# Six adaLN vectors move out of the two mixers and into the FFN blocks of a two-layer hybrid decoder

## The chip, the cores and the metric

The kernel runs on one NeuronCore of one Trainium2 chip. The metric is the time of one execution in microseconds (us); the time before is the median of 3 runs. An engine takes its instructions in order: PE is TensorE's matmul (PEld its weight load), DVE VectorE, ACT ScalarE, POOL GpSimd, SP the engine that issues most DMAs.

## The reference, cut to what matters

Two layers of three sub-layers: FFN, mixer, FFN. Each sub-layer has three vectors of 1024 numbers, shift, scale and gate, that come out of one condition vector `c`:

```python
for l in range(DEPTH):                       # 2 layers
    mod = (silu(c) @ ada_w[l] + ada_b[l]).reshape(Bn, N_SUB, 3, D_MODEL)
    shift, scale, gate = mod[:, :, 0], mod[:, :, 1], mod[:, :, 2]
    # sub-layer s = 0 and 2: y = swiglu(h, w1, w3, w2); s = 1: y = hybrid_mixer(h, ...)
    h = x * (1 + scale[:, s]) + shift[:, s]
    x = layer_norm(ALPHA * x + weight * (1 + gate[:, s]) * y, ln_g[l, s], ln_b[l, s])
```

`x` is 512 x 1024, the FFN is 2816 wide, everything is f32. That makes 18 vectors (2 layers, 3 sub-layers, 3 each), each a product of the 1024 numbers silu(c) with a 1024 x 1024 piece of `ada_w` (4 MB).

## The kernel before, in words

**Products.** A weight tile of 128 x 1024 is loaded (`raw`), cut into a high part (`whi`, ACT, L103) and the rest (`wlo`, DVE, L105), and each product takes three matmuls, high x high, low x high, high x low (L121 to L123, in `mm3`). Activations are cut in the same way (`hT_hi` and `hT_lo`).

**FFN block** (`ffn`). 22 tiles of hidden units in two halves of 11. For each tile an up step: two weight tiles, 48 matmuls of 512 columns (`h`), and the gated product on ACT and DVE (L310 to L316). Then the down steps: for each hidden tile one weight tile times the gate row `G` (L101), cut and used in 24 matmuls (`y`). `bg()` is called after each step: it makes the next pieces of background work.

**Mixer** (`mixer`). Input projections (`tA`, `tB`, `pj`), the state-space part, compression (`hid`), then the attention stage: for 24 units (`p`, query block, branch) scores `S`, a softmax on DVE and ACT, four transposes into `tp` (L921), a copy of `tp` by ACT into `pt` (L923), and the product of `pt` with the values into `op` (L931). A list of `jobs` (projections, then the output product `y`) is put between them by `tick`; `part` and `rest` are the output product and the closing norm of a block of 128 tokens.

**adaLN vectors** (`ada_vec`). A vector takes 8 loads of 512 KB (in_ada_w) and 8 products with reduction on DVE (L156, a "dot"): a tile of weights times the row `csil` (silu of c, made by `silu_c` on ACT L146 and DVE L147). Its 8 columns are then joined with the bias. A gate vector goes to DRAM and comes back as a row `G` on all partitions (L190, L192); scale and shift go with the norm's gains into `GA` and `BB` (`next_par`, L204 to L206), which `spread` uses to make the next sub-layer's `hT` (ACT L226 and L228, DVE L224 and L229). The first two vectors are made in `feed`; the other 16 in the order of the list `order`: gate of a sub-layer, then scale and shift of the next. `share` says how many of them each sub-layer makes: 4, 3, 3, 3, 3. In an FFN block a vector's tiles are buffers of the pool `bp` (8 of 4 KB a partition, also used by `lg`, `lb`, `G`, `z`), loaded one ahead; in a mixer they are the same 4 `raw` buffers as the weights'. `make_bias` (the table of position biases, which the mixer reads as `T` from DRAM, `lane`) is run in the first FFN ahead of the last vector there. The mixer forgets `csil` before it begins and makes it again in the attention stage.

**Order of work.** A scheduler lays the instructions of each engine in a fixed order when the program is built: an instruction may be far ahead of the place where the code calls it. PE follows that order and waits where an operand is late.

Of the kernel before, what the change touches and what calls it, by code (L numbers as in the profile page):

```python
# [51 lines left out]
def kernel(ctx: ExitStack, tc: tile.TileContext, a: dict, out: bass.AP,  # L52
                             subs=((0, 0), (0, 1), (0, 2), (1, 0), (1, 1), (1, 2))):
# [23 lines left out]
    def big(s):  # L77
        return bp.tile([128, 1024], F32, tag="b", name=nm(s))

    def tiny(s, n, dt=F32):  # L80
        rot = s in ("mx", "sm", "fc", "st", "mv", "rs", "nr", "gst", "ss")
        return (t4 if rot else t1).tile([128, n], dt, tag=f"t_{s}", name=nm(s))
# [4 lines left out]
    def load(dst, src):  # L87
        nc.sync.dma_start(dst, src)

    def bcast_row(src, n):  # L90
        return bass.AP(tensor=src.tensor, offset=src.offset, ap=[[0, 128], [1, n]])
# [51 lines left out]
    def silu_c():  # L143
        csil, c_th = big("csil"), big("cth")
        load(csil, bcast_row(a["c"][0], 1024))
        S.activation(c_th, csil, AF.Tanh, scale=0.5)  # L146
        V.scalar_tensor_tensor(csil, c_th, 1.0, csil, op0=ALU.add, op1=ALU.mult)  # L147
        cond["c"] = csil
# [10 lines left out]
    def ada_fetch(l, s, j, k):  # L159
        raw = big("raw0")  # L160
        load(raw, a["ada_w"][l, s * 3 + j, k])
        return raw

    def ada_vec(l, s, j, ahead=None, follow=None):
        acc, ab = tiny(nm("mod"), 8), tiny("ab", 8)
        load(ab, a["ada_b"][l, s * 3 + j])
        for k in range(8):
            if ahead is None:
                raw = wp.tile([128, 1024], F32, tag="raw", name=nm("raw"), bufs=4)
            else:  # L170
                raw = ahead.pop(0)
                if k < 7:
                    ahead.append(ada_fetch(l, s, j, k + 1))
                elif follow:
                    ahead.append(ada_fetch(*follow, 0))
            ada_dot(acc, raw, l, s * 3 + j, k, ahead is None)
            yield
        if j == 0:
            V.tensor_add(acc, acc, ab)
        else:  # L180
            V.scalar_tensor_tensor(acc, acc, 1.0, ab, op0=ALU.add, op1=ALU.add)
        mods[l, s, j] = acc
        if j == 2:
            d = dram.tile([1, 1024], F32, tag=nm("mod"), name=nm("mod"))
            load(bass.AP(tensor=d.tensor, offset=d.offset, ap=[[1, 128], [128, 8]]), acc)
            mods[l, s, j] = d

    def gate_par(l, s, P):
        g = P["G"] = big("G")
        load(g, bcast_row(mods[l, s, 2][0], 1024))  # L190
        if s != 1:
            V.tensor_scalar(g, g, 0.25, None, op0=ALU.mult)  # L192

    def norm_par(l, s, P):
        P["lg"], P["lb"] = big("lg"), big("lb")
        load(P["lg"], bcast_row(a["ln_g"][l, s], 1024))
        load(P["lb"], bcast_row(a["ln_b"][l, s], 1024))

    def next_par(l, s, nl, ns, P):
        GA, BB = P["GA"], P["BB"] = tiny("GA", 8), tiny("BB", 8)  # L200
        load(GA, a["lng_c"][l, s])
        load(BB, a["lnb_c"][l, s])
        sc, sh = mods[nl, ns, 1], mods[nl, ns, 0]
        V.tensor_mul(GA, sc, GA)  # L204
        V.tensor_mul(BB, sc, BB)
        V.tensor_add(BB, BB, sh)  # L206
# [227 lines left out]
    def mixer(l, P, last, lane, bg, gate_params, norm_params):  # L434
# [440 lines left out]
        def score(p, qb, br, rate):  # L875
            if p not in lanes:
                lane_load(p)
            if br == 0:
                return score_c(p, qb)
            nk = (qb + 1) * 128  # L880
            per = 2 if nk <= 256 else 1
            qs = slice(qb * 128, (qb + 1) * 128)
            mx, sm = tiny("mx", 4), tiny("sm", 4)
            pr = []
            for e, (g, i) in enumerate(heads(p)):
                if e % per == 0:
                    ps, pt = bank("S", "S"), slab("P", "P")
                cols = slice(e % per * nk, (e % per + 1) * nk)
                o, w = ps[:, cols], pt[:, cols]
                PE.matmul(o, Q[g, i][:, qs], K[br][0][g][:, :nk], start=True, stop=False)  # L890
                PE.matmul(o, Q[g, i][:, qs], K[br][1][g][:, :nk], start=False, stop=True)  # L891
                m = mx[:, e:e + 1]
                V.tensor_tensor_reduce(out=w, in0=o, in1=lanes[p][e][:, 512 - nk:], scale=-1.0, scalar=3.0e38,
                                       op0=ALU.add, op1=ALU.min, accum_out=m)
                S.activation(w, w, AF.Exp, bias=m, scale=-1.0, accum_out=sm[:, e:e + 1])
                pr.append(w)
                tick(rate)
            factor(sm, p, qb, br)
            for e in range(4):
                if (br, e) in ACT_SCALE:  # L900
                    S.activation(pr[e], pr[e], AF.Copy, scale=sm[:, e:e + 1])
                else:
                    V.tensor_scalar(pr[e], pr[e], sm[:, e:e + 1], None, op0=ALU.mult)
            return pr
# [100 lines left out]
                    jobs.pop(0)  # L1005
            credit[0] = min(credit[0], 1)

        silu_c()
        probs = [score(*u, TICK_0) for u in units[:LOOK]]
        for n, (p, qb, br) in enumerate(units + [(2, 0, 0)]):  # L1010
            if n + LOOK < len(units):
# [55 lines left out]
    lane = []  # L1067

    order = []
    for n, (l, s) in enumerate(subs):  # L1070
        order.append((l, s, 2))
        if n + 1 < len(subs):
            order += [(*subs[n + 1], 1), (*subs[n + 1], 0)]
    share = {0: 4, 1: 3, 2: 3, 3: 3, 4: 3}

    def need(*key):
        if key not in mods:
            if "c" not in cond:
                silu_c()
            for _ in ada_vec(*key):  # L1080
                pass

    def make_bg(n, P):
        l, s = subs[n]
        items = [k for k in order if k not in mods][:share.get(n, 0)]
        total = 9 * len(items) + (8 if n == 0 else 0) + (s != 1)
        slots = {0: 34, 1: 18, 4: 18}.get(n, 36)
        early = 10 if n == 0 else 0
        done = [0, 0]

        def parts():
            ahead = None
            if s != 1 and items:
                ahead = [ada_fetch(*items[0], 0)]
                yield
            for key, follow in zip(items, items[1:] + [None]):
                yield from ada_vec(*key, ahead, follow)
                if key == (l, s, 2):
                    gate_par(l, s, P)
                if n + 1 < len(subs) and key == (*subs[n + 1], 0):  # L1100
                    next_par(l, s, *subs[n + 1], P)
                yield
                if n == 0 and key == items[-2]:
                    yield from make_bias()

        gen = parts()

        def bg(more=False):
            done[0] += 0 if more else 1
            k = early // 2  # L1110
            even = 2 * done[0] if done[0] <= k else early + (done[0] - k) * (total - early) // (slots - k)
            want = done[1] + 1 if more else min(total, even)
            while done[1] < want:
                done[1] += 1
                next(gen, None)

        return bg

    for n, (l, s) in enumerate(subs):
        last = n == len(subs) - 1  # L1120
        P = {}

        def params():
            norm_par(l, s, P)
            if (l, s, 2) in mods:
                gate_par(l, s, P)
            if not last and (*subs[n + 1], 0) in mods:
                next_par(l, s, *subs[n + 1], P)

        if s == 1:  # L1130
            if not lane:
                for _ in make_bias():
                    pass
            need(l, s, 2)
            cond.clear()
            mixer(l, P, last, lane, make_bg(n, P), lambda: gate_par(l, s, P), lambda: norm_par(l, s, P))
        else:
            if share.get(n) and "c" not in cond:
                silu_c()
            after_mixer = n > 0 and subs[n - 1][1] == 1  # L1140
            ffn(l, s, P, last, make_bg(n, P), (2, 0) if after_mixer and QORDER[0] == 3 else (0, 2), params,
                feed if n == 0 else None)
# [87 lines left out]
```

## Time and profile before

| what | value |
|---|---|
| median of 3 runs | 2078.81 us (2078.62 to 2080.05) |
| the profiled execution's own time | 2078.53 us |
| its span | 2076.8 us, mean granted TensorE clock 0.998 |
| first FFN block, up to the first mixer | 0 to about 388 us |
| first mixer (attention from about 512) | 388 to about 694 us |
| second and third FFN block | 694 to 1045, 1045 to 1410 us |
| second mixer (attention from about 1534) | 1410 to about 1716 us |
| last FFN block | 1716 to 2077 us |

How to read the profile: a row of the stretches gives busy time and number of instructions (in brackets) of PE, PEld, DVE, ACT and POOL, then the granted TensorE clock, the share of the DMA engines' time and GB/s. A row of the timeline gives start, duration, engine, line, operation, what it writes and reads, form, number, and in square brackets idle time before it with what ended it. Matmuls overlap: each is shown with about 0.39 us, and one starts every 0.23 us. So PE's pace is read from starts and not from durations. "issue" is time in which the engine waited for nothing that the profile shows.

### The profile page before, as it was taken

How to read it: one execution, taken by the hardware profiler on the slowest of the kernel's cores; microseconds unless marked ns; L12 is line 12 of the kernel's file. 1: busy time of each engine (PE TensorE's matmuls, PEld its weight loads, DVE VectorE, ACT ScalarE, POOL GpSimd, SP SyncE). 2: the span in 40 equal slices, each digit the busy share in tenths (PEclk: the TensorE clock that was granted, in tenths of full speed). 3: DMA queues.
4: the chain of work that ended last, by engine and by line, in shares of the span. 5: the costliest groups of instructions: out<-in, count | busy, mean ns of one | idle time of the engine just before them, and what ended most of it. 6: DMA issues, size and time to landing. Idle time of an engine off the chain costs nothing.

```text
span 2076.8 us, 25951 instructions
## 1 busy us (share of the span) xinstructions
PE 2037.8 (98%) x10024; PEld 1652.0 (80%) x10024; DVE 1330.7 (64%) x2425; ACT 770.2 (37%) x1352; POOL 27.8 (1%) x43
## 2 busy tenths in 40 slices
PE   6999999999999999999999999999999999999997
PEld 5888888887666888888888888888776678888886
DVE  6784455778898875334696534468788984444454
ACT  3321223525556422222343222235356673222322
POOL 0000000000000000000000000000000000000000
PEclk9999999999999999999999999999999999999999
DMA  9662633235353763332566333143254523233321
GB/s 359 225 232 83 213 122 124 74 99 173 126 169 92 260 201 108 93 100 61 172 231 185 93 100 98 65 144 102 92 172 129 176 79 125 81 112 93 100 92 41
DMA packets 93144, 280.26 MB, mean 135 GB/s; under 512 B 19251, under 2 KB 23603, under 8 KB 93020
## 3 DMA queue, kind: packets, MB, share of 16 engines
q1 hardware_dynamic: 92348, 275.95, 40.6%
q0 software_dynamic: 672, 2.64, 0.4%
q8 instruction: 79, 1.29, 0.3%
q14 instruction: 45, 0.37, 0.1%
HBM read 276.41 MB, written 4.76 MB: 135 GB/s over the span
## 4 chain that ended last, share of the span: by engine, by line
PE 90%; DVE 5%; ACT 2%; issue 1%; DMA 1%; POOL 0%; SPq 0%; POOLq 0%; ACTq 0%
PE h L121 15%; PE h L122 15%; PE h L123 15%; PE y L121 8%; PE y L123 8%; PE y L122 8%; PE pj L121 3%; PE pj L122 3%; PE pj L123 3%; PE op L931 3%; PE tp L921 2%; PE S L890 1%; DVE raw L156 1%; PE S L891 1%; PE hid L624 1%
## 5 line engine op out<-in xcount | busy, mean ns | idle before, releaser
L103 ACT CAST whi<-raw 128x1024 fp32r<-128x1024 f32 (+1 forms) x306 | 316.8, 1046 | 719.4 <-issue 353.8
L121 PE MATMUL h<-hT_hi,whi 128*128 128x512 f32 (+1 forms) x1488 | 559.1, 377 | 4.5 <-ACT hT_hi L1064 4.4
L122 PE MATMUL h<-hT_lo,whi 128*128 128x512 f32 (+1 forms) x1488 | 559.1, 376 | 0.0
L123 PE MATMUL h<-hT_hi,wlo 128*128 128x512 f32 (+1 forms) x1488 | 558.9, 376 | 0.0
L105 DVE TENSOR_TENSOR wlo<-raw,whi 128x1024 fp32r<-128x1024 f32 (+1 forms) x306 | 369.4, 1215 | 232.8 <-ACT whi L103 232.4
L121 PEld LDWEIGHTS h<-hT_hi,whi 128*128 128x128 f32 x1488 | 280.1, 188 | 56.0 <-ACT hT_hi L1064 5.4
L123 PEld LDWEIGHTS h<-hT_hi,wlo 128*128 128x128 f32 x1488 | 280.4, 188 | 50.8
L122 PEld LDWEIGHTS h<-hT_lo,whi 128*128 128x128 f32 x1488 | 280.5, 188 | 50.5 <-DVE hT_lo L1065 0.2
L121 PE MATMUL y<-whi,ghi 128*128 128x512 f32 x576 | 224.1, 389 | 0.0
L122 PE MATMUL y<-wlo,ghi 128*128 128x512 f32 x576 | 224.1, 389 | 0.0
L123 PE MATMUL y<-whi,glo 128*128 128x512 f32 x576 | 224.1, 389 | 0.0
L156 DVE CUSTOM_DVE_ANT_0 raw<-raw,csil 128x1024 f32<-128x1024 f32 x144 | 173.7, 1218 | 22.9 <-DMA raw<-in_ada_w_dram 22.4
L312 DVE TENSOR_TENSOR th<-th,h 128x512 f32<-128x512 f32 x88 | 60.2, 685 | 147.3 <-PE h L123 146.9
L101 DVE TENSOR_TENSOR raw<-raw,G 128x1024 f32<-128x1024 f32 x86 | 104.9, 1221 | 66.8 <-DMA raw<-in_w_dram 66.3
L123 PEld LDWEIGHTS y<-whi,glo 128*128 128x128 f32 x576 | 108.1, 188 | 22.5
L121 PEld LDWEIGHTS y<-whi,ghi 128*128 128x128 f32 x576 | 108.1, 188 | 22.5
L122 PEld LDWEIGHTS y<-wlo,ghi 128*128 128x128 f32 x576 | 108.1, 188 | 22.4
L121 PE MATMUL pj<-hT_hi,whi 128*128 128x512 f32 x288 | 117.3, 407 | 0.0
L122 PE MATMUL pj<-hT_lo,whi 128*128 128x512 f32 x288 | 113.7, 395 | 0.0
L123 PE MATMUL pj<-hT_hi,wlo 128*128 128x512 f32 x288 | 113.3, 393 | 0.0
L315 ACT CAST ghi<-th 128x512 fp32r<-128x512 f32 x88 | 54.5, 620 | 145.7 <-DVE th L312 145.7
L311 DVE SCALAR_TENSOR_TENSOR th<-th,h 128x512 f32<-128x512 f32 x88 | 59.9, 681 | 44.9 <-ACT th L310 44.8
(291 smaller groups left out, 2552.4 us busy)
## 6 DMA issues: line engine op xcount, KB each, us to landing
raw<-in_w_dram SPq DMA_DIRECT2D x264, 512.0 KB, 3.6
raw<-in_ada_w_dram SPq DMA_DIRECT2D x144, 512.0 KB, 5.5
raw<-in_wS_dram SPq DMA_DIRECT2D x36, 512.0 KB, 3.5
raw<-in_cw_dram SPq DMA_DIRECT2D x16, 512.0 KB, 3.7
raw<-in_wo_dram SPq DMA_DIRECT2D x16, 512.0 KB, 4.2
T<-lane SPq DMA_DIRECT2D x16, 256.0 KB, 3.7
lg<-in_ln_g_dram SPq DMA_DIRECT2D x6, 512.0 KB, 4.6
lb<-in_ln_b_dram SPq DMA_DIRECT2D x6, 512.0 KB, 3.8
```

Of the source, the lines that this page charges most:

```text
L101: V.tensor_mul(raw, raw, gain)
L103: S.copy(hi[:, :n], raw[:, :n])
L105: V.tensor_sub(lo[:, :n], raw[:, :n], hi[:, :n].bitcast(F32))
L121: PE.matmul(o, lh, rh, start=first, stop=False)
L122: PE.matmul(o, lh, rl, start=False, stop=False)
L123: PE.matmul(o, ll, rh, start=False, stop=last)
L156: V.tensor_tensor_reduce(out=raw, in0=raw, in1=cond["c"], scale=0.5, scalar=0.0, op0=ALU.mult, op1=ALU.add, accum_out=acc[:, k:k + 1])
L311: V.scalar_tensor_tensor(th, th, 1.0, h1, op0=ALU.add, op1=ALU.mult)
L312: freed[0] = V.tensor_mul(th, th, h3).ins
L315: S.copy(hi, th)
L921: PE.transpose(tp[0:n, e * 128:(e + 1) * 128], pr[e][:, kb * 128:kb * 128 + n], ident)
L931: PE.matmul(op[r, :], v, pt[0:n, g * 256:(g + 1) * 256], start=(br == 0), stop=(br == 2 and kb == qb))
```

## The change

`share` becomes 6, 5, 5 for the first, second and third FFN block; both mixers make none, and the last FFN block makes none as before. The order of the list stays. So these vectors change place (layer, sub-layer, kind):

- scale and shift of (0, 2): from the first mixer to the first FFN block; `make_bias` now runs after five vectors there and not after three.
- gate of (0, 2): from the first mixer to the second FFN block, which uses it itself.
- scale of (1, 1): from the third FFN block to the second.
- gate of (1, 2), scale and shift of (1, 2): from the second mixer to the third FFN block.

The mixer no longer calls `silu_c`; the second FFN block does, since it finds no `csil`. `GA` and `BB` for the sub-layer after a mixer are now made in the mixer's step for the norm's parameters.

```diff
@@ mixer
-        silu_c()
         probs = [score(*u, TICK_0) for u in units[:LOOK]]
@@
-    share = {0: 4, 1: 3, 2: 3, 3: 3, 4: 3}
+    share = {0: 6, 2: 5, 3: 5}
@@
             need(l, s, 2)
             cond.clear()
-            mixer(l, P, last, lane, make_bg(n, P), lambda: gate_par(l, s, P), lambda: norm_par(l, s, P))
+
+            def last_params():
+                norm_par(l, s, P)
+                next_par(l, s, *subs[n + 1], P)
+
+            mixer(l, P, last, lane, make_bg(n, P), lambda: gate_par(l, s, P), last_params)
```

On PE the order within the FFN blocks stays but for the two small matmuls of `make_bias`; in the attention stages it changes. Two places, before and now.

First PE in the first mixer's attention, the same unit of scores in both (`tp` transposes of scaled scores `P`, `op` the product with values `vS`, `S` scores, `y` output product). Before:

```order
L921 MATMUL tp_5156<-cst,P_4958 128x128
L931 MATMUL op_5083<-pt_5144,vS_2879 64x256 x2
L921 MATMUL tp_5156<-cst,P_4964 128x128
L921 MATMUL tp_5156<-cst,P_4970 128x128
L921 MATMUL tp_5156<-cst,P_4976 128x128
L921 MATMUL tp_5165<-cst,P_4958 128x128
L921 MATMUL tp_5165<-cst,P_4964 128x128
L921 MATMUL tp_5165<-cst,P_4970 128x128
L921 MATMUL tp_5165<-cst,P_4976 128x128
L121 MATMUL y_5327<-whi_4632,hT_hi 128x512
L931 MATMUL op_5083<-pt_5161,vS_2879 64x256 x2
L931 MATMUL op_5083<-pt_5170,vS_2879 64x256 x2
```

The same four-transpose groups with the change:

```order
L921 MATMUL tp_5145<-cst,P_4976 128x128
L921 MATMUL tp_5145<-cst,P_4982 128x128
L921 MATMUL tp_5154<-cst,P_4964 128x128
L921 MATMUL tp_5154<-cst,P_4970 128x128
L921 MATMUL tp_5154<-cst,P_4976 128x128
L921 MATMUL tp_5154<-cst,P_4982 128x128
L890 MATMUL S_5165<-kh_3633,qa_4510 128x384
L891 MATMUL S_5165<-kl_3636,qa_4510 128x384
L890 MATMUL S_5171<-kh_3633,qa_4620 128x384
L891 MATMUL S_5171<-kl_3636,qa_4620 128x384
L931 MATMUL op_5078<-pt_5150,vS_2935 64x256 x2
L931 MATMUL op_5078<-pt_5159,vS_2935 64x256 x2
```

Where one output matmul stood between the transposes and the products that need their copies, four score matmuls stand now.

Then ACT at the start of the second FFN block (`hsum` and `hT_hi` are the last token block's input, `cth` the tanh of `silu_c`), with the change:

```order
L226 ACTIVATE hsum_5796<-hps_5786,BB_4643,GA_4642 128x128 x4
L226 ACTIVATE hsum_5803<-hps_5791,BB_4643,GA_4642 128x128
L228 CAST hT_hi<-hsum_5796 128x512
L226 ACTIVATE hsum_5803<-hps_5791,BB_4643,GA_4642 128x128 x2
L146 ACTIVATE cth_5819<-csil_5818 128x1024
L228 CAST hT_hi<-hsum_5803 128x512
L103 CAST whi_6051<-raw_6049 128x1024
L310 ACTIVATE th_6055<-h_1067_5847 128x512
```

The tanh now stands ahead of the cast that ends the block's input.

DVE at the same place before (`G` the gate row, `raw_1096` the first dot's weights):

```order
L229 TENSOR_TENSOR hT_lo<-hsum_5831,hT_hi 128x512
L156 ISA raw_1096_6101,mod_1112_6180<-raw_1096_6101,csil_3916 128x1024
L156 ISA mod_1112_6180 128x1
L224 TENSOR_SCALAR hsum_5838<-hps_5826,GA_5043,BB_5044 128x128
L229 TENSOR_TENSOR hT_lo<-hsum_5838,hT_hi 128x512
L192 TENSOR_SCALAR G_6107<-G_6107 128x1024
```

And now:

```order
L229 TENSOR_TENSOR hT_lo<-hsum_5796,hT_hi 128x512
L224 TENSOR_SCALAR hsum_5803<-hps_5791,GA_4642,BB_4643 128x128
L147 SCALAR_TENSOR_TENSOR csil_5818<-cth_5819,csil_5818 128x1024
L229 TENSOR_TENSOR hT_lo<-hsum_5803,hT_hi 128x512
L156 ISA raw_1080_6063,mod_1085_6073<-raw_1080_6063,csil_5818 128x1024
L156 ISA mod_1085_6073 128x1
```

The first dot went behind the block's last input, and the product that makes `csil` took its place; the gate row is no longer at hand here.

## The prediction

> **What bounds the kernel now.** First the page: busy time, then the chain of work that ended last.
>
> ```profile
> span 2076.8 us, 25951 instructions
> PE 2037.8 (98%) x10024; PEld 1652.0 (80%) x10024; DVE 1330.7 (64%) x2425; ACT 770.2 (37%) x1352; POOL 27.8 (1%) x43
> PE 90%; DVE 5%; ACT 2%; issue 1%; DMA 1%; POOL 0%; SPq 0%; POOLq 0%; ACTq 0%
> ```
>
> PE is the bound, but its busy time overlaps itself, so I look at the stages. These stretches are, in this order, the second FFN block, the fronts of the second and third FFN block, and the attention stages of the two mixers (PE, PEld, DVE, ACT, POOL, clock, DMA share, GB/s).
>
> ```profile
> 694.00:1030.00 336.00, 335.89 (x1523) 279.72 (x1522) 184.28 (x229) 94.59 (x116) 0.55 (x1) 1.00 0.44 143
> 700.00:760.00 60.00, 60.00 (x285) 50.46 (x284) 53.02 (x84) 19.17 (x25) 0.00 (x0) 1.00 0.81 282
> 1054.00:1114.00 60.00, 60.00 (x329) 52.45 (x329) 53.55 (x86) 19.46 (x27) 0.00 (x0) 1.00 0.83 297
> 512.00:672.00 160.00, 157.88 (x900) 109.34 (x898) 143.14 (x451) 98.37 (x250) 2.78 (x3) 1.00 0.41 129
> 1534.00:1695.00 161.00, 159.44 (x905) 110.22 (x904) 144.32 (x452) 99.23 (x253) 2.77 (x3) 1.00 0.41 130
> ```
>
> In the FFN block PE is never idle (335.89 of 336.00) and DVE has 184.28 of 336 us to do. In attention DVE has 143.14 of 160 us, 89%, and PE is idle for 2.12 and 1.56 us. So the work that moves leaves the stages where DVE is fullest, and the question is what PE loses there to late operands. Third the waits, of PE alone, in the whole run and then in the two mixers' later parts (500 to 694, 1523 to 1716):
>
> ```profile
> PE hps L1041 <- DMA x_sb<-in_x_dram: 12.0, 2, 9.8
> PE h L121 <- ACT hT_hi L1064: 4.4, 3, 2.4
> PE hps L215 <- ACT z L269: 4.1, 5, 1.4
> PE op L931 <- ACT pt L923: 3.2, 7, 0.8
> PE y L121 <- ACT hsum L226: 1.3, 2, 0.7
> ...
> PE op L931 <- ACT pt L923: 1.9, 4, 0.8
> PE y L121 <- ACT hsum L226: 0.7, 1, 0.7
> ...
> PE op L931 <- ACT pt L923: 1.3, 3, 0.8
> PE y L121 <- ACT hsum L226: 0.7, 1, 0.7
> ```
>
> The largest rows belong to the start of the kernel (`hps` on `x_sb`, `h` on L1064) and to the seams of the blocks, which the change does not touch. In the mixers PE never waits for DVE's scaled scores. It waits for ACT's copies `pt`, 3.2 us in 7 places. That is small beside the 48 dots of 1.22 us (58 us, rows below) that leave.
>
> **The change, part by part.** *The dots.* What stands in the mixers now, in instructions of L156 on DVE by stretch (two instructions a dot), and how long one is:
>
> ```profile
> 512.00:672.00 160.00, 26.24 (x44) 1.00 0.41 129
> 1534.00:1695.00 161.00, 26.78 (x44) 1.00 0.41 130
> L156 DVE CUSTOM_DVE_ANT_0 raw<-raw,csil x144: 1191/1218/1228, 11.0 to 1670.4; 128x1024 f32<-128x1024 f32 x144
> L146 ACT ACTIVATE cth<-csil x3: 1057/1062/1065, 6.0 to 1526.7; 128x1024 f32<-128x1024 f32 x3
> L147 DVE SCALAR_TENSOR_TENSOR csil<-cth,csil x3: 1216/1219/1226, 7.1 to 1528.4; 128x1024 f32<-128x1024 f32 x3
> ```
>
> A mixer loses three vectors, 24 dots of 1.22 us (22 of them in the stretch above, 26.24 us), and one `silu_c`, 1.06 us of ACT and 1.22 of DVE. DVE in attention falls from 143 to 117 of 160 us. PE does the same matmuls, so none of this is a gain by itself; only PE's waits are.
>
> *Where they go.* Each of the first three FFN blocks gets 16 more dots: 16 x 1.22 = 19.5 us of DVE and 8 MB of loads. The cover is PE's own length: 184 + 20 of 336 us. The fronts show the densest mixture there is, DVE 53.02 of 60 us at 282 GB/s with PE at 60.00 of 60; now this lasts for 40 dots and not for 24, at the front's rate (24 dots in about 63 us) some 105 us and not 63, within the first half's up steps (11 tiles of 48 matmuls at 0.23, 120 us). I take 0 us. Bounds: nothing below zero, since PE has no wait in there to lose; above, 2 us, if one down step starves.
>
> *The gate of (0, 2) is now made in the block that uses it.* A store, a load back and a wait of DVE at L192, with the gated products queued behind it. The first block already does this:
>
> ```profile
> DVE G L192 <- DMA G<-mod: 10.7, 3, 6.7
> 34.00:140.00 106.00, 106.00 (x477) 87.78 (x475) 81.16 (x131) 32.73 (x44) 0.00 (x0) 1.00 0.76 268
> ```
>
> Its wait of 6.7 us lies in that stretch, and PE is busy for 106.00 of 106: weight tiles cut one hidden tile ahead (48 x 0.23 = 11 us of PE) cover it. 0 us; if the cover were gone it would cost up to 6.7.
>
> *`silu_c` at the seam.* On SP its load takes the place of the first dot's load; on ACT its tanh stands ahead of the last cast of the block's input, on DVE its product ahead of the last `hT_lo`. Before, this place looks so:
>
> ```profile
> 686.39 0.42 SPq L88 DMA_DIRECT2D raw<-in_ada_w_dram  x1
> 692.33 1.23 DVE L156 CUSTOM_DVE_ANT_0 raw<-raw,csil 128x1024 f32<-128x1024 f32 x1
> 693.93 0.62 ACT L228 CAST hT_hi<-hsum 128x512 fp32r<-128x512 f32 x1 [1.66 <-DVE hsum L224]
> 694.58 0.69 DVE L229 TENSOR_TENSOR hT_lo<-hsum,hT_hi 128x512 fp32r<-128x512 f32 x1 [0.69 <-ACT hT_hi L228]
> csil<-in_c_dram SPq DMA_DIRECT2D x3, 512.0 KB, 5.1
> DMA to landing us min/median/max: 3.4/4.4/9.8
> ```
>
> The dot waited for its load until 692.33 and held `hsum` and so the cast at 693.93. With 5.1 us from the end of the issue (686.8) `csil` lands at 691.9; tanh from about 692.3 to 693.4, then the cast, to 694.0 against 694.55 before; DVE's product from 693.4 to 694.6, then `hT_lo`, as before at 694.6. So 0 us, perhaps 0.5 gained. If the load takes the 9.8 us that a row of `G` once took (last line), it lands at 696.6 and `hT_hi` is ready at 698.3: 3.8 us lost, the upper bound.
>
> [...]
>
> *`make_bias` later.* The order has 240 PE rows more ahead of it, 240 x 0.23 = 55 us. 0 us by the next lines: its matmuls were at 236, now about 291, and the first `T` is read at 384.
>
> ```profile
> 236.08 1.17 PE rowps L416 x4
> L88 SPq DMA_DIRECT2D T<-lane x16: 319/369/384, 384.4 to 1622.1; - x16
> ```
>
> *PE's order in attention.* This is the only term that I count. How it looks in the timeline of PE in the first mixer, at the longest wait, at an undisturbed place and at the place shown in the order:
>
> ```profile
> 562.97 0.28 PE L891 MATMUL S<-kl,qa 128*128 128x256 f32 x1
> 564.09 0.65 PE L931 MATMUL op<-pt,vS 128*64 128x256 f32 x4 [0.84 <-ACT pt L923]
> ...
> 584.59 0.39 PE L122 MATMUL y<-wlo,hT_hi 128*128 128x512 f32 x1
> 584.81 0.39 PE L123 MATMUL y<-whi,hT_lo 128*128 128x512 f32 x1
> 585.13 0.65 PE L931 MATMUL op<-pt,vS 128*64 128x256 f32 x4
> ...
> 619.61 0.98 PE L921 MATMUL tp<-cst,P 128*128 128x128 f32 x7
> 620.35 0.48 PE L121 MATMUL y<-whi,hT_hi 128*128 128x512 f32 x1
> 620.89 1.14 PE L931 MATMUL op<-pt,vS 128*64 128x256 f32 x8
> ```
>
> From `y` to `y` it takes 0.22 to 0.23 us, from `y` to `op` 0.32 (584.81 to 585.13). At the last place it takes 0.54: one matmul was not enough to hide ACT's copy, and PE lost 0.2 without being shown as idle. In that mixer I find three such places of 0.2 beside the 1.9 us of shown waits, so 2.5 us; in the second 1.3 + 0.6 = 1.9. In the new order four score matmuls of 384 columns, 0.23 x 384 / 512 = 0.17 us each, stand at that place. Along the whole order, with these starts and 0.74 / 7 = 0.1 us for a transpose (619.61 to 620.35), by my estimate 4 of a mixer's 48 copies now have under 0.8 us between their transposes and their product, against 9. The place at 564.09, 0.84 us, stays: there the order still has only two score matmuls between. So the gain is (2.5 - 0.84) + (1.9 - 0.84) = 2.7 us. Bounds: 0, if as many new waits come; 5.7, if all waits for `pt` and `hsum` and the six small ones go (3.2 + 1.3 + 1.2).
>
> *Sum.* 0 + 0 + 0 + 0 - 2.7: the profiled execution, 2078.53 us (span 2076.8 and 1.7 around it), would become 2075.8. The median lies 0.28 us above it: 2076.1 us.
>
> **The rivals.** About 0.2%, 4.2 us, is what a measurement of this kernel can tell from no change; my forecast is inside that.
>
> *Forecast, 0.50.* The mixers' waits shrink by 0 to 5.7 us, the FFN blocks hide the dots. A third of this case is beyond 4.2 (0.18): the upper bound is, and the order has fewer breaks between kinds of matmul, which I cannot price.
>
> *A: nothing, 0.22.* PE's work is the same and the new order makes as many short waits as it removes. For it: PE never waited for the dots. 2078.8, within 1.5 us.
>
> *B: slower, 0.13.* With DVE freed the scheduler sets products earlier than ACT's copies come, on this chip and not in its plan. One such place costs 0.84 us as at 564.09; eight more in each mixer are 13 us, less the 2.7: 2089; it is slower by over 0.2% from five in each. Against it: the new order leaves more between transposes and products, not less.
>
> *C: larger, 0.15.* With DVE at 73% all of attention moves up: scores, copies and the seam's waits come early, so the 5.7 us go, and the seam's 4.1 us on `z` partly. 8 us: 2070.8. For it: DVE is at 89% there, and what ACT has ahead of a copy may wait for DVE.
>
> **How the numbers follow.** Faster by over 0.2%: 0.18 + 0.15 = 0.33. Slower: 0.13. Within: 0.32 + 0.22 = 0.54. The range leaves out most of B and the far end of C, less than 0.2 together: from 2070.5 to 2081.0.
>
> **What would show it.** Right: no L156 in the mixers and DVE near 117 of 160 us there; PE's waits for `pt` half as long; `hT_hi` at the seam at its old distance from the first `h`; PE 100% in the fronts with dots for about 105 us. Wrong: a PE wait in an FFN block, above all for `whi` in a down step; a wait of tanh on `csil` at the seam with PE idle behind it; or the attention stage shorter by more than 3 us a mixer with the same waits, which would mean that the order and not the waits set it.

## The result, and the profile after

The changed kernel takes 2100.91 us (median of 4 runs, 2100.01 to 2103.02) against 2078.72 us for the kernel before in the same runs: 1.0108 times as long, 95% interval 1.0095 to 1.012. I had predicted 2076.1 us. The profiled execution has a span of 2099.0 us, 22.2 more than before. First the page: span, busy time and the chain of work that ended last.

```profile
span 2099.0 us, 25917 instructions
PE 2042.4 (97%) x10024; PEld 1655.1 (79%) x10024; DVE 1345.1 (64%) x2424; ACT 769.1 (37%) x1351; POOL 27.8 (1%) x43
...
PE 83%; DVE 7%; DMA 5%; ACT 2%; issue 2%; POOL 0%; SPq 0%; POOLq 0%; ACTq 0%; DVEq 0%
```

The number of matmuls is the same, but PE's share of the chain fell from 90% to 83%, and DMA's rose from 1% to 5%: somewhere the end of the kernel now hangs on loads and on DVE. Next, what PE waited for, over the whole run (us in total, times, longest):

```profile
PE y L121 <- DVE th L312: 17.7, 3, 8.1
PE hps L1040 <- DMA x_sb<-in_x_dram: 12.2, 2, 9.9
...
PE h L121 <- ACT hT_hi L228: 0.8, 1, 0.8
PE op L931 <- ACT pt L923: 0.7, 2, 0.4
```

The first row is new. L312 is the second product of the gated unit on DVE and the last reader of the banks of `h`, and those banks are handed on to `y`. So the wait stands where an FFN block turns from up steps to down steps. The last row shows that the mixers did improve: the waits for `pt` fell from 3.2 us to 0.7.

Where the time went by stage I read from PE's first `y` after `h` and first `h` after `y` (143.4, 203.3, 324.3 us and so on before). Stages not listed differ by 0.2 us at most.

| stage | before | after | difference |
|---|---|---|---|
| first block, first half's down steps | 59.8 | 69.6 | +9.8 |
| from its second half's down steps through the first mixer to the first `h` behind | 354.9 | 353.5 | -1.4 |
| second block, first half's up steps (with the seam) | 123.2 | 124.4 | +1.2 |
| second block, first half's down steps | 59.8 | 72.7 | +12.9 |
| third block, first half's down steps | 59.8 | 59.8 | 0.0 |
| from the third block's second half's down steps through the second mixer | 354.1 | 353.6 | -0.5 |

That is +22.0 of the 22.2 us. The whole loss stands at two turns. The same stretches as windows, the three blocks' first down steps in the changed kernel (PE, PEld, DVE, ACT, POOL, clock, DMA share, GB/s):

```profile
143.58:213.20 69.62, 61.52 (x265) 50.53 (x264) 45.28 (x61) 13.82 (x15) 0.00 (x0) 0.95 0.57 172
812.20:884.90 72.70, 63.11 (x265) 51.24 (x265) 40.06 (x47) 14.86 (x16) 0.00 (x0) 0.93 0.35 119
1190.60:1250.40 59.80, 59.80 (x265) 49.53 (x264) 29.09 (x29) 13.77 (x14) 0.00 (x0) 1.00 0.29 97
```

The matmuls are as many in each, 265; in the first two DVE has 61 and 47 instructions and not 29, PE is idle for 8.1 and 9.6 us and the mean granted clock is 0.95 and 0.93. Now DVE at the first turn, before the change:

```profile
137.92 1.22 DVE L156 CUSTOM_DVE_ANT_0 raw<-raw,csil 128x1024 f32<-128x1024 f32 x1
...
142.93 0.68 DVE L311 SCALAR_TENSOR_TENSOR th<-th,h 128x512 f32<-128x512 f32 x1
143.72 0.69 DVE L312 TENSOR_TENSOR th<-th,h 128x512 f32<-128x512 f32 x1
```

and with it:

```profile
146.44 1.22 DVE L156 CUSTOM_DVE_ANT_0 raw<-raw,csil 128x1024 f32<-128x1024 f32 x1
...
147.59 0.68 DVE L311 SCALAR_TENSOR_TENSOR th<-th,h 128x512 f32<-128x512 f32 x1
148.19 1.22 DVE L156 CUSTOM_DVE_ANT_0 raw<-raw,csil 128x1024 f32<-128x1024 f32 x1
...
151.99 1.23 DVE L156 CUSTOM_DVE_ANT_0 raw<-raw,csil 128x1024 f32<-128x1024 f32 x1 [0.75 <-DMA raw<-in_ada_w_dram]
...
153.15 0.68 DVE L312 TENSOR_TENSOR th<-th,h 128x512 f32<-128x512 f32 x1
```

Before, the last dot of this half starts at 137.92 and the last L312 at 143.72. Now 50 dots stand ahead of the last L312 in DVE's order and not 41 (16 of them are `feed`'s in both), and L312 starts at 153.15, 9.4 us later. Nine dots at 1.15 us from start to start are 10.3 us. PE had nine `y` matmuls to do in banks that were free, then nothing.

In the second block DVE's rows at the turn look different:

```profile
807.88 1.23 DVE L156 CUSTOM_DVE_ANT_0 raw<-raw,csil 128x1024 f32<-128x1024 f32 x1 [3.50 <-DMA raw<-in_ada_w_dram]
...
812.67 1.23 DVE L156 CUSTOM_DVE_ANT_0 raw<-raw,csil 128x1024 f32<-128x1024 f32 x1 [3.56 <-DMA raw<-in_ada_w_dram]
...
813.82 0.68 DVE L311 SCALAR_TENSOR_TENSOR th<-th,h 128x512 f32<-128x512 f32 x1
```

DVE is not full here. Two dots wait 7.06 us for loads, and the gated products, long ready, stand behind them. The DMA engines in these microseconds:

```profile
800.00:803.00 3.00, 3.00 (x15) 2.48 (x14) 3.00 (x5) 1.12 (x2) 0.00 (x0) 1.00 1.04 279
803.00:806.00 3.00, 3.00 (x15) 2.49 (x14) 1.38 (x2) 0.00 (x0) 0.00 (x0) 1.00 1.36 53
806.00:809.00 3.00, 3.00 (x15) 2.49 (x14) 1.12 (x1) 0.00 (x0) 0.00 (x0) 1.00 0.67 33
```

From 803 us on they are busy with 33 to 53 GB/s. What SP had issued, from its timeline:

```profile
799.79 0.38 SPq L88 DMA_DIRECT2D mod<-mod  x1
...
802.67 0.33 SPq L88 DMA_DIRECT2D raw<-in_w_dram  x1
803.04 14.76 SPq L88 DMA_DIRECT2D raw<-in_ada_w_dram  x5
```

`mod<-mod` is the store of a finished gate vector, here that of (1, 0): 4 KB, 1024 numbers. From 801 to 803 us 1205 packets of under 512 B pass. Before, this store went out at 757 us, when the block's dots were done.

### The profile page after: what moved, and what is told of

Same layout as the page of the kernel before. It is cut to its first block, busy times and chain, and to the rows that moved or that the text cites. A ratio compares the mean times of both kernels' runs of the same rounds, so it can differ in the third digit from the quotient of the medians.

```text
span 2099.0 us, 25917 instructions
## 1 busy us (share of the span) xinstructions
PE 2042.4 (97%) x10024; PEld 1655.1 (79%) x10024; DVE 1345.1 (64%) x2424; ACT 769.1 (37%) x1351; POOL 27.8 (1%) x43
## 4 chain that ended last, share of the span: by engine, by line
PE 83%; DVE 7%; DMA 5%; ACT 2%; issue 2%; POOL 0%; SPq 0%; POOLq 0%; ACTq 0%; DVEq 0%
PE h L122 12%; PE h L121 12%; PE h L123 12%; PE y L123 8%; PE y L121 8%; PE y L122 8%; PE pj L121 3%; PE pj L122 3%; PE pj L123 3%; PE op L931 3%; DMA raw<-in_ada_w_dram 3%; PE tp L921 2%; DVE raw L156 2%; PE S L890 1%; DVE wlo L105 1%
## 5 line engine op out<-in xcount | busy, mean ns | idle before, releaser
L121 PE MATMUL y<-whi,ghi 128*128 128x512 f32 x576 | 226.2, 393 | 17.7 <-DVE th L312 17.7
L156 DVE CUSTOM_DVE_ANT_0 raw<-raw,csil 128x1024 f32<-128x1024 f32 x144 | 173.5, 1221 | 38.7 <-DMA raw<-in_ada_w_dram 37.8
L312 DVE TENSOR_TENSOR th<-th,h 128x512 f32<-128x512 f32 x88 | 60.2, 685 | 135.2 <-PE h L123 134.9
L101 DVE TENSOR_TENSOR raw<-raw,G 128x1024 f32<-128x1024 f32 x86 | 104.9, 1221 | 46.2 <-DMA raw<-in_w_dram 45.7
L923 ACT COPY pt<-tp 128x512 f32<-128x512 f32 (+2 forms) x96 | 54.3, 581 | 67.1 <-PE tp L921 65.3
```

Source lines behind the costliest of these rows:

```text
L101: V.tensor_mul(raw, raw, gain)
L121: PE.matmul(o, lh, rh, start=first, stop=False)
L156: V.tensor_tensor_reduce(out=raw, in0=raw, in1=cond["c"], scale=0.5, scalar=0.0, op0=ALU.mult, op1=ALU.add, accum_out=acc[:, k:k + 1])
L312: freed[0] = V.tensor_mul(th, th, h3).ins
L923: S.copy(pt[0:n, :], tp[0:n, :])
```

## The experiments

Theory 1: the loss is at the turn of the first half in two blocks, because the fixed order of DVE has dots ahead of the last gated products and these dots are late there; late either because DVE has too much (1a) or because loads come late (1b). Rivals: the loads and dots cost time wherever they stand in the FFN blocks; the gate that the second block must now make for itself (a wait at L192); the mixers' new order. All times below are medians; "loss" at a turn is that stage's length less that of before (59.8 us), read from the one profiled execution of each kernel. The second block is the same in the changed kernel, e10 and e11 and lost 12.9, 11.4 and 13.7 us, so a difference of 2 us between two losses is not read as an effect. The kernel before took 2079.04 us beside e1 to e4, 2078.87 beside e5 to e8 and 2078.75 beside e9 to e12.

**e1: vectors held back to the second half.**

```diff
 # up steps of a half
-                    bg()
+                    if half == 0:
+                        bg()
+                    else:
+                        with tc.issue_after(freed[0]):   # DVE: behind the last gated product
+                            bg()
 # down steps: no bg() any more
 # make_bg (slots and early are gone)
+        ups = 7 if n == 0 else 10
+        first = 9 * {0: 4, 2: 3, 3: 3}.get(n, 0) + (s != 1)
+            even = first * c // ups if c <= ups else first + (total - first) * (c - ups) // 10
```

> The changed kernel, but each block makes only as many vectors ahead of its turn from up steps to down steps as before (four, three, three); the other six are made in the second half's up steps, each dot behind the gated product ahead of it on DVE. All 16 vectors are made, none in the mixers. Theory 1 (the loss is dots that stand ahead of the last gated products at the turn of the first half): the waits of y for L312 (17.7 us) and the slow matmuls behind them go, 9.7 us in the first and 12.9 us in the second block; 2076 to 2080 us. Rival (48 more dots in the FFN blocks cost time wherever they stand there): over 2090 us, with waits in the second halves.

Measured: 2092.14 us, ratio 1.0067 (1.0055 to 1.008). The second block's loss is gone, from 12.9 to 0.0. The first block's is not: 13.7 us, and 2.0 in its up steps. Half of the expectation failed. DVE and SP at that turn:

```profile
144.80 0.68 DVE L311 SCALAR_TENSOR_TENSOR th<-th,h 128x512 f32<-128x512 f32 x1
154.70 2.59 DVE L101 TENSOR_TENSOR raw<-raw,G 128x1024 f32<-128x1024 f32 x2 [9.22 <-DMA raw<-in_w_dram]
157.21 0.68 DVE L312 TENSOR_TENSOR th<-th,h 128x512 f32<-128x512 f32 x1
```

```profile
140.08 0.38 SPq L88 DMA_DIRECT2D mod<-mod  x1
140.55 4.70 SPq L88 DMA_DIRECT2D raw<-in_w_dram  x3
```

No dot is in the way now. My edit had put the fourth vector, the gate of (0, 1), whole ahead of the turn (before, it was made behind it), and its store went out at 140.08. The three loads of weights issued behind the store landed 11.9 us after their issue (median), and DVE stood 9.22 us in L101 with L312 queued behind. So a gate's store near the turn can hold up the products with no dot in the way; that it does so in the changed kernel is for e5 to show. That 48 more dots cost time wherever they stand is ruled out by the second and third block: their second halves take 16 dots each without a loss.

**e2: the mixers' half alone.** `share` is 4, 3, 3 for the FFN blocks, and the six vectors that the mixers made are dropped from `order`; the mixer's own three take the places of those of the sub-layer behind it.

```diff
-    share = {0: 6, 2: 5, 3: 5}
+    share = {0: 4, 2: 3, 3: 3}
+    left_out = ((0, 2, 1), (0, 2, 0), (0, 2, 2), (1, 2, 1), (1, 2, 0), (1, 2, 2))
+    order = [k for k in order if k not in left_out]
...
+            for j in range(3):                     # ahead of each mixer
+                mods[l, 2, j] = mods[l, 1, j]
```

> The mixers' half of the change alone: no dots and no silu_c in the mixers, 4, 3 and 3 vectors in the FFN blocks; the six vectors that the mixers made are left out (the other layer's sub-layer's are used in their place), so it shows what leaving is worth without what arriving costs. By the prediction's step on PE's order in attention: 2.7 us less than before, 2076.1 us. By the stage account of the changed kernel (first mixer 1.5 us shorter, second 0.5, the seam behind the first 1.2 longer): 0.8 us less, 2078.0 us. If the loss sat in the new attention order: over 2085.

Measured: 2078.36 us, ratio 0.9997 (0.9988 to 1.0006). By stages: first mixer -1.4 us, second -0.4, the seam behind the first +2.5, the turns 0.0: 0.7 us more in the profiled execution, which took 2079.26 us; the median is 0.7 us less, inside the interval. So leaving the mixers is worth 1.8 us, and in this execution `silu_c` at the seam took it back.

**e3 and e4: the moved vectors' dots cut short, or their loads left out.**

```diff
 # e3, for the six vectors that moved
+        m = 128 if (l, v // 3, v % 3) in EXTRA else 1024
+        V.tensor_tensor_reduce(out=raw[:, :m], in0=raw[:, :m], in1=cond["c"][:, :m], ...
 # e4, for the same
+        if (l, s, j) not in EXTRA:
             load(raw, a["ada_w"][l, s * 3 + j, k])
+        in0 = cond["c"] if (l, v // 3, v % 3) in EXTRA else raw   # of the dot
```

> The changed kernel, with the dots of the six vectors that moved cut to 128 of 1024 columns (their loads stay whole, the rest of each product is left out). DVE is relieved of some 1 us in each of 48 dots, the DMA engines of nothing. Theory 1a (DVE has too much ahead of the turn): the wait at the first block's turn, 8.3 us, falls below 2, and the second's 10.2 below 4; 2078 to 2085 us. Theory 1b (the dots wait for loads that come late, and the products stand behind them): the second block keeps its 10 us, the first loses some; 2090 to 2096 us.

> The changed kernel, but the six vectors that moved are not loaded (their dots multiply the row csil with itself, as long as before), so DVE has all its work and the DMA engines 24 MB less. Theory 1a (DVE's amount): 2096 to 2101 us, both stalls there. Theory 1b (late loads): the second block's stall of 10 us goes, 2086 to 2091 us; if the first's goes too, 2078.

Measured: e3 2096.38 us (1.0084, 1.0065 to 1.0102), e4 2096.03 (1.0082, 1.0064 to 1.01). The losses are 11.5 and 8.8 us in e3, 11.0 and 9.8 in e4. Neither settles what I asked. In the first block I had cut the wrong vectors: of the nine more dots ahead of its turn seven belong to the gate of (0, 1), which this block made before as well, and only two to a vector that I had cut. In the second block the loss stays with short dots and without loads, since it passes to whatever waits for a load behind the store, in e4 the weights. DVE in e4 (L102 there is L101):

```profile
812.64 1.23 DVE L102 TENSOR_TENSOR raw<-raw,G 128x1024 f32<-128x1024 f32 x1 [7.09 <-DMA raw<-in_w_dram]
```

**e5: without two stores of gates.** The mixer's gate row and the third block's are those of their neighbours.

```diff
         mods[l, s, j] = acc
-        if j == 2:
+        if (l, s, j) == (0, 1, 2):
+            mods[l, s, j] = mods[0, 0, 2]
+        elif (l, s, j) == (1, 0, 2):
+            mods[l, s, j] = mods[0, 2, 2]
+        elif j == 2:
```

> The changed kernel without the stores of two gate rows, those of (0, 1) and (1, 0), which are sent out near the turn of the first and of the second block (149.6 and 799.8 us); the rows of (0, 0) and (0, 2) are used in their place. The order on DVE and PE is that of the changed kernel. If the store (4 KB in over a thousand small packets, with the DMA engines at 1.0 and 33 to 53 GB/s for some 12 us behind it) is what made the second block's dots wait 3.50 and 3.56 us: 7 us less and the first block as it was, 2092 to 2095 us. If DVE's amount of work sets the turn: as the changed kernel, 2100 us.

Measured: 2093.34 us (1.0071, 1.0048 to 1.0094). The second block's loss falls from 12.9 to 4.7; the first's is 11.3. The order of DVE and PE is the changed kernel's, so the store alone is worth 8.2 us there. In the first block the store is not the cause: its loss stays. The DMA engines in the same microseconds as above:

```profile
803.00:806.00 3.00, 3.00 (x15) 2.49 (x14) 3.00 (x6) 0.00 (x0) 0.00 (x0) 1.00 0.84 250
806.00:809.00 3.00, 3.00 (x15) 2.49 (x14) 1.52 (x2) 0.00 (x0) 0.00 (x0) 1.00 0.94 336
```

DVE at that turn in e5 (L316 there is L312), the second-last and the last gated product and the third dot between them:

```profile
811.55 0.68 DVE L316 TENSOR_TENSOR th<-th,h 128x512 f32<-128x512 f32 x1
...
815.04 1.22 DVE L156 CUSTOM_DVE_ANT_0 raw<-raw,csil 128x1024 f32<-128x1024 f32 x1
...
817.17 0.69 DVE L316 TENSOR_TENSOR th<-th,h 128x512 f32<-128x512 f32 x1
```

Three dots (812.15, 813.90, 815.04) stand between the two products without a wait for a load, and PE waits once there, 2.7 us, for the second product (of its two waits for L316, 11.7 us, the other is 9.0).

**e6: no wait of DVE for the gate row.** The factor 0.25 is put on the 128 x 8 numbers ahead of the store, and L192 is gone.

```diff
 # gate_par
-        if s != 1:
-            V.tensor_scalar(g, g, 0.25, None, op0=ALU.mult)
 # ada_vec, ahead of the store
+            if s != 1:
+                V.tensor_scalar(acc, acc, 0.25, None, op0=ALU.mult)
```

> The changed kernel with the factor 0.25 of the gate applied to the vector of 128 x 8 before the store, so that no instruction of DVE waits for the row G (L192 is gone); everything is computed. In the changed kernel DVE waited there 7.9 us in the first and 10.5 us in the second block, with dots behind it. If that wait is what pushes the dots into the turn: both turns are 8 to 10 us earlier on DVE, the stalls go, 2078 to 2083 us. If the dots are paced by their loads and catch up anyway: within 3 us of the changed kernel, 2098 to 2101 us.

Measured: 2100.37 us (1.0102, 1.0073 to 1.0131): losses of 8.2 and 14.4 us. The rival of the gate falls. What DVE no longer waited for `G` it waited for loads instead, between 700 and 826 us:

```profile
DVE raw L156 <- DMA raw<-in_ada_w_dram: 17.7, 11, 10.3
```

In the changed kernel this row reads 12.2 us, with 10.5 for `G` beside it; the waits of L101 for weights went from 0.4 to 4.8 us.

**e7 and e8: one block alone,** by two other lists in `share`.

```diff
-    share = {0: 6, 2: 5, 3: 5}
+    share = {0: 6, 1: 1, 2: 3, 3: 3, 4: 3}   # e7
+    share = {0: 4, 1: 3, 2: 5, 3: 3, 4: 1}   # e8
             cond.clear()
+            if share.get(n):
+                silu_c()
...
```

A mixer that makes vectors calls `silu_c` ahead of all its work, where the kernel before called it in the attention stage. The rest of the edit makes `GA` and `BB` in the mixer's last step only if their vectors are there.

> Six vectors in the first block as with the change, one in the first mixer, three, three and three in the later stages: the other blocks have their old vectors. All vectors are made. Theory 1: the first block loses 9.7 us as with the change and the others nothing, less up to 1 us in the first mixer: 2087 to 2089 us. If the loss in the first block comes from the whole program's new order: 2079.

> Five vectors in the second FFN block, as with the change, but four in the first block, three in the first mixer (the gate of (0, 2) and the silu of c are made there, as before), three in the third block and one in the second mixer. All vectors are made. Theory 1 (the number of dots ahead of the turn): the second block loses some 10 to 13 us, 2088 to 2092 us. If what counts is that this block must first make its own gate and csil (DVE waits 10.5 us for G and 1.8 for the tanh): it loses under 3 us, 2078 to 2081 us.

Measured: e7 2092.55 us (1.0065, 1.0042 to 1.0087), a loss of 10.0 us at the first turn and none at the second. e8 2082.07 us (1.0016, 1.0004 to 1.0027), no loss at either turn. In both, the mixer that makes one vector is longer, by 4.2 and 4.8 us; this belongs to my edit and not to the question. PE waits there once, in both alike:

```profile
PE S L890 <- DVE Pc L863: 4.1, 1, 4.1
```

So e7 is as theory 1 has it. e8 speaks against its simple form: 40 dots ahead of the second block's turn cost nothing where this block has neither its own gate nor `csil` to make and the gate of (1, 0) is stored at 752.97 us, far from the turn.

**e9: three vectors ahead of each turn.** As e1, but for one number.

```diff
-        first = 9 * {0: 4, 2: 3, 3: 3}.get(n, 0) + (s != 1)
+        first = 9 * {0: 3, 2: 3, 3: 3}.get(n, 0) + (s != 1)
```

> As the kernel with held vectors, but the first block makes only three vectors ahead of its first turn and three in its second half (and so three and three, three and two, three and two). Two things change at the first turn: 8 dots fewer stand ahead of it, and the store of the gate of (0, 1), which went out at 140.1 us there, comes in the second half. All vectors are made, none in the mixers. If the two causes found (dots on DVE ahead of the turn, and a gate's store close ahead of it) are all: no wait of y for L312, 59.8 us from the first turn to the second half as before, and 2 us less than before from the mixers: 2076 to 2078 us. If 24 dots in the second half cost there: over 2080.

Measured: 2077.84 us, ratio 0.9996 (0.9987 to 1.0005), as expected. Both turns lose nothing; the mixers give 1.4 and 0.5 us, the seam takes 1.2. At the first turn DVE now waits for PE:

```profile
140.67 0.68 DVE L311 SCALAR_TENSOR_TENSOR th<-th,h 128x512 f32<-128x512 f32 x1
144.10 0.69 DVE L312 TENSOR_TENSOR th<-th,h 128x512 f32<-128x512 f32 x1 [2.75 <-PE h L123]
```

All 16 vectors are made in the FFN blocks here, as with the change. This kernel beats the changed one by 1.1% and cannot be told from the one before.

**e10 and e11: the first block's last three vectors, with short dots or without loads.** The edits of e3 and e4 with another list.

```diff
-EXTRA = ((0, 2, 1), (0, 2, 0), (1, 0, 2), (1, 1, 1), (1, 2, 1), (1, 2, 0))
+EXTRA = ((0, 1, 2), (0, 2, 1), (0, 2, 0))
```

> The changed kernel, with the dots of the first block's last three vectors, (0, 1) gate, (0, 2) scale and shift, cut to 128 of 1024 columns; their loads stay whole. These, not the ones cut before, are the dots that stand ahead of the last products at the first turn. If DVE's amount of work is the cause there: the first block's 9.8 us fall below 2, the second block keeps its 12.9, 2090 to 2093 us. If loads are: the first block keeps over 8 us, 2098 to 2101.

> The changed kernel, but the first block's last three vectors are not loaded, their dots as long as before (csil times itself). DVE's amount: the first block keeps over 8 us, 2098 to 2101 us. Loads: it falls below 2, 2090 to 2093 us.

Measured: e10 2099.17 us (1.0097, 1.0079 to 1.0116), e11 2103.27 (1.0117, 1.0098 to 1.0135). The first block loses 8.1 and 11.8 us. Neither cure works alone, and the rows say why. DVE in e10, where a dot takes 0.29 us but waits for its load:

```profile
144.97 0.29 DVE L158 CUSTOM_DVE_ANT_0 raw<-raw,csil 128x128 f32<-128x128 f32 x1 [0.98 <-DMA raw<-in_ada_w_dram]
...
146.25 0.29 DVE L158 CUSTOM_DVE_ANT_0 raw<-raw,csil 128x128 f32<-128x128 f32 x1 [0.98 <-DMA raw<-in_ada_w_dram]
```

and in e11, where there is nothing to wait for:

```profile
145.42 1.22 DVE L157 CUSTOM_DVE_ANT_0 raw<-csil 128x1024 f32<-128x1024 f32 x1
...
146.56 1.22 DVE L157 CUSTOM_DVE_ANT_0 raw<-csil 128x1024 f32<-128x1024 f32 x1
```

In e10 a dot starts every 1.28 us, when its load has come; in e11 every 1.14, one behind the other. Ahead of the first turn loads and dots have almost the same pace, so 1a and 1b were a false choice: what counts is that nine more dots (ten in e11) stand ahead of the products, not which of the two makes them slow. Both cures at once were not run.

**e12: without the two stores and without L192.** The edits of e5 and e6 together.

> The changed kernel without the stores of the gates of (0, 1) and (1, 0), and with the factor 0.25 applied before the store of the others, so that DVE never waits for G. Without these stores the second block lost 4.7 us of its 12.9. If the 4.7 is the wait for G (10.5 us on DVE, early in the block): it goes, the second block loses under 1 us and the first some 10, 2088 to 2090 us. If it is the number of dots: 4 to 5 us stay, 2092 to 2094 us.

Measured: 2094.42 us (1.0074, 1.0056 to 1.0093). The second block loses 5.7 us, the first 9.6. So the 4.7 us that e5 left are not the wait for `G`. Beside e6, which has both stores and no L192 either, the second block loses 8.7 us less: a second measure of what the store costs there.

## Why the prediction was wrong

*Dots and `silu_c` leave the mixers, no gain by itself: right.* No L156 is left in the attention stages. DVE there has 124.5 of 160 us (520.4 to 680.4), not the 117 that I had by subtraction. The 22 dots are gone from it, but the busy time is 7.6 us above the difference. The other instructions are not longer: added up row by row they take 148.6 us before and 147.6 now. Rows on DVE overlap (a dot of 1.22 us starts 1.15 after the last), so taking one busy time from the other took off too much.

*Where they go: this step failed.* I took 0 us, with 2 as the upper bound; it was 9.8 in the first and 12.9 in the second block, 0.0 in the third. Two things were wrong with it. First, the cover: I set DVE's 204 us against PE's 336 and the dense front's 105 us against the 120 us of up steps. But PE's length covers late DVE work only while PE has other work in its order, and at the turn it has nine `y` matmuls (six in the second block), 2.2 us or less. So the front must end ahead of a fixed point, and 15 us of room is what the estimate had to prove. Second, the rate: 24 dots in 63 us left out what the change itself adds ahead of the turn. DVE in the second block, its first dot, its wait for the gate row and its 24th dot:

```profile
704.83 1.22 DVE L156 CUSTOM_DVE_ANT_0 raw<-raw,csil 128x1024 f32<-128x1024 f32 x1
...
744.11 0.69 DVE L192 TENSOR_SCALAR G<-G 128x1024 f32<-128x1024 f32 x1 [10.53 <-DMA G<-mod]
...
781.07 1.22 DVE L156 CUSTOM_DVE_ANT_0 raw<-raw,csil 128x1024 f32<-128x1024 f32 x1
```

From the first to the 24th it took 76 us, and the store of the next gate came at 799.79. In the first block the front was no front at all: with the 16 dots of `feed` it was full from the start, and the new vectors went straight to the turn. I had the order that says so: with the change DVE has seven dots between the last two L312 of the half. I read the order of PE in the attention stage and not that of DVE at the turns.

In the third block the 0 held, with the same 40 dots ahead of the turn. Its gate is the last of its five vectors: the store goes out at 1186.02, 4.6 us ahead of the turn at 1190.58, but no dot stands behind it, SP issues no load until 1195.51, and the last L312 waits 2.21 us for PE and not PE for it. So of the stores near the turns of the second and the third block the one with needed loads behind it cost time (8.2 us, e5), and the one with none behind it cost none.

*The gate of (0, 2) made in its own block: the wait was right, the price elsewhere.* DVE waits 10.5 us at L192, PE loses nothing behind it, and taking the wait away gains nothing (e6). But making a gate also issues a store, and a store close ahead of the turn costs 8.2 us in this block (e5). I had weighed the wait and not the queue that the moved store goes through. The harm is done by the gate of (1, 0), which the change pushed from the third to the fourth place in its block.

*`silu_c` at the seam: mechanism right, size off.* I took 0 with a bound of 3.8. The seam is 1.2 us longer with the change and 2.5 in e2. ACT with the change:

```profile
702.00 1.06 ACT L146 ACTIVATE cth<-csil 128x1024 f32<-128x1024 f32 x1 [1.19 <-DMA csil<-in_c_dram]
702.96 0.60 ACT L228 CAST hT_hi<-hsum 128x512 fp32r<-128x512 f32 x1
```

The load was issued at 694.95 and landed 7.0 us after its issue, not 5.1; the cast behind the tanh came late, and PE waited 0.8 us for it. The cast's last input was ready at 701.25 (DVE L224), but the cast started at 702.96, behind the tanh, which had waited 1.19 us for `csil`.

Eleven kernels have this seam (the changed one, e1 to e6 and e9 to e12). In their profiled executions the load landed 5.8 to 8.3 us after its issue, and in each the seam was longer by what the landing took beyond 5.8 us, to 0.1 us: 0.0 at 5.8 (e12), 1.2 at 7.0, 2.5 at 8.3 (e2). So the price is the lateness of this one load, as in the prediction's upper bound; what failed was the landing of 5.1 us taken from the kernel before, which none of the eleven reached. Two slips in the working are smaller: 5.1 us counts from the start of an issue and was added to its end, and by the prediction's own steps the upper bound is 4.2 us and not 3.8.

*`make_bias` later: 0, right.* No stage behind it is longer.

*PE's order in attention: right in sign, 1.9 us and not 2.7.* The two stages with the mixers are 1.4 and 0.5 us shorter (0.4 in the second in e2), inside the bounds of 0 to 5.7; the waits for `pt` fell by 2.5 us.

*The rivals.* B, the only slower one, put the loss into the attention stages; they got shorter. None had the turn. The line of the prediction on what would show it wrong, a PE wait in an FFN block, did, though for `th` and not for `whi`.

What stays open: the 4.7 us that the second block loses without the store. The wait for `G` is not it (e12), and 40 dots without `csil` and the gate in front lose nothing (e8), where no dot stands between the last two gated products. The rows of e5 point to the three dots that stand there, some 3.4 us at 1.15 each. In the changed kernel PE waits twice at this turn, 5.60 us for the product behind the late loads and 3.98 us for the one behind these dots. That these dots are late because the block starts them later fits, but no run took these three away alone, so it is not shown.

## What to carry to other kernels

PE, busy for 97% of the span, hid late work of DVE only as long as its own fixed order had something else to do: at the two turns nine and six matmuls, 2.2 us or less. In another kernel look for the points where the busiest engine has nothing else to do (here the change from up to down products, where banks are handed on) and count, in the queue of the engine it waits for, what stands ahead of the one instruction it needs. Background work should be kept off such points by order, not by its average share: the same 16 vectors in the same blocks cost 22 us in one order and nothing in another (e9). And with a step that is moved its small stores are moved too (one of 4 KB cost 8.2 us here, e5): look at what is loaded behind them.

## What the runs showed of the hardware

*Loads behind a store of 4 KB landed 12 us after their issue.* DMA in the changed kernel from 800 to 812 us, and in e5, which leaves the store out:

```profile
DMA packets 1589, 1.49 MB, mean 124 GB/s; under 512 B 1228, under 2 KB 1228, under 8 KB 1589
```

```profile
DMA packets 1165, 3.72 MB, mean 310 GB/s; under 512 B 260, under 2 KB 260, under 8 KB 1164
```

With the store, 968 more small packets pass and 1.49 MB; without it, 3.72 MB. Loads of 512 KB issued in this window landed 12.1 to 12.5 us after their issue with the store (medians), and 6.0 to 6.9 without. In the kernel before, loads behind the same store landed after 11.4 us and cost nothing, some 45 us ahead of the turn. A stored vector has 1024 numbers; over the whole run e5, with two stores fewer, has 2079 fewer packets under 512 B. In the kernel before, the 4 us from the store's issue on (757 to 761) show 1184 packets, all under 512 B, with 0.01 MB in all.

*The two turns lost 22.7 us, PE's waits there are 17.7.* PE behind the first turn, and the stretch of the granted clock (0.51) from 150 to 155 us:

```profile
153.88 0.79 PE L121 MATMUL y<-whi,ghi 128*128 128x512 f32 x1 [8.10 <-DVE th L312]
...
155.33 0.63 PE L121 MATMUL y<-whi,ghi 128*128 128x512 f32 x1
155.75 0.63 PE L122 MATMUL y<-wlo,ghi 128*128 128x512 f32 x1
156.18 0.63 PE L123 MATMUL y<-whi,glo 128*128 128x512 f32 x1
...
157.68 0.40 PE L122 MATMUL y<-wlo,ghi 128*128 128x512 f32 x1
157.91 0.39 PE L123 MATMUL y<-whi,glo 128*128 128x512 f32 x1
```

```profile
150.00:155.00 5.00, 1.12 (x3) 0.93 (x4) 4.24 (x7) 0.62 (x2) 0.00 (x0) 0.51 0.94 173
```

After the wait a matmul starts every 0.42 us for some 3 us, then every 0.23 again. PE's waits for L312 add up to 17.7 us, the two stages lose 22.7 us; the slow matmuls are a part of what lies between. PE had been idle for 8.10 us ahead of them, and the mean granted clock was 0.51 from 150 to 155 us and 0.81 from 155 to 160.
